# A conformer block, a matrix-memory mixer and a gated recurrence in one kernel: two branches of the mixer in seven-product pairs, its output gates first, some remainders by adding DMAs

## The chip, the cores and the metric

The kernel runs on one core of one Trainium2 chip. The metric is the device time of one execution in microseconds (us), the median of a few runs. TensorE multiplies matrices, VectorE (DVE) and ScalarE (ACT) work element by element, GpSimd (POOL) does a few special steps and issues the adding DMAs, and SyncE (SP) issues most of the other DMAs.

## The reference

512 tokens of width 1024 go through a conformer block (a gated feed-forward layer, a mixer with two kinds of attention, a second feed-forward layer, a norm) and then through two recurrent layers: a matrix-memory mixer (mLSTM, four heads) and a gated linear recurrence. All is float32. The change lies in the matrix memory, of which this is the part that matters (`u` is the normed input):

```python
def mlstm_mixer(u, w_in, conv_w, conv_b, w_q, w_k, w_v, b_i, b_f, norm_w, skip, w_out):
    proj = u @ w_in
    xm, z, o_pre, i_pre, f_pre = jnp.split(proj, [M_INNER, 2 * M_INNER, 3 * M_INNER, 3 * M_INNER + M_HEADS], axis=-1)
    xc = jax.nn.silu(causal_dwconv(xm, conv_w, conv_b))
    # per head of 512 columns: q, k (256 wide) from xc, v (512 wide) from xm
    h_tilde = mlstm_chunkwise(q, k, v, log_i, log_f)
    hh = sigmoid(o_pre) * h_tilde
    hn = layernorm(hh) * norm_w                  # over the 512 columns of a head
    y = (hn + skip * xc) * jax.nn.silu(z)
    return y @ w_out
```

Here `w_in` is 1024 by 6152, so x, z and o take 512 columns each in every one of the four heads.

## The kernel before

Activations lie transposed: a tile holds 128 features by 512 tokens. A float32 product is made of three single-pass ones: each operand is split into a part `hi` that TensorE's fast float32 format holds exactly and a remainder `lo`, and `mm3` (lines 112 to 115) issues hi by hi, hi by lo and lo by hi. A weight is brought by `wload` (lines 93 to 101): SP loads it into `raw` (128 by 1024, four buffers), ScalarE rounds it into `hi` (line 98), VectorE subtracts for `lo` (line 100); `hi` and `lo` have five buffers each. One such load serves 24 matmuls of 512 columns.

The feed-forward layers already use the class `Pair` and `pair_products` (lines 225 to 341). There two groups of 128 output columns are treated as a two-by-two product of blocks and computed with seven block products instead of eight. The inputs' sums come once from `xhalves` and its `step(k)` (lines 266 to 293), which leaves 28 tiles of 128 by 512 to be kept. The weights' sums come for each pair from a DMA that adds (line 214, issued by GpSimd), two VectorE additions (lines 249 and 250) and splits (lines 220, 222, 258, 260). Each of the seven products is 12 matmuls of 256 columns, and VectorE joins them (lines 325 to 337). While one pair is multiplied, the next is loaded and split.

In the matrix memory, `mlstm` (lines 708 to 987), no pairs are used. For each head `z_proj` and `x_proj` run four plain groups each (a group is 24 matmuls of 512 columns), `o_proj` 96 matmuls of 512 columns for the output gate, `v_proj` 48, `qk_proj` 48, `out_proj` 96; `scores` and `numer` are the chunk's attention-like part, `x_conv` the convolution, `y_out` the gating (transposes and elementwise work). The order is written out by hand at lines 960 to 987: head 0 is opened, then each of three passes runs scores, o (or v), numer, z of the next head, y_out, x and v of the next head, x_conv, out_proj (in the third pass o of head 3), q and k; a tail finishes head 3.

A scheduler orders each engine's instructions by this order, by priorities (`tc.high_priority` moves an instruction ahead by so many places) and by when they can run, and gives tiles their buffers. Long-lived tiles come from the pool `ap` (40 buffers), shorter ones from `xp` (18, through `ctile`), and double tiles from `gp` (2, twice as large).

## Time and profile before

| | |
|---|---|
| median of 3 runs | 1811.5 us (1811.38 to 1811.58) |
| the profiled execution's own time | 1811.49 us |
| span of its instructions | 1809.8 us |
| mean granted TensorE clock | 0.998 |

The span runs from the first to the last instruction; 1.7 us of the time lie around it. In the profile an engine's busy time counts the time in which at least one of its instructions runs. TensorE's matmuls overlap, so the distance between two starts tells their pace, and not the duration that is listed for one.

### The profile page before, as it was taken

What the parts mean: (1) busy time and instruction counts of PE and PEld (TensorE: products, weight loads), DVE (VectorE), ACT (ScalarE), POOL (GpSimd) and SP (SyncE); (2) the same over time, 40 slices, a digit from 0 to 9 for tenths busy, and PEclk for the clock granted to TensorE, in tenths of its full rate; (3) what the DMA queues carried; (4) which work ended last, traced back from release to release, by engine and by line L of the source; (5) the groups of instructions that cost most, each with busy time, mean ns of one, the idle gap of its engine ahead of it and who ended that gap; (6) DMA issues with size and microseconds to landing.
All of it is one profiled execution on the core that took longest, in us unless ns stands there. A gap on an engine that the chain in (4) does not pass through costs nothing.

```text
span 1809.8 us, 24643 instructions
## 1 busy us (share of the span) xinstructions
PE 1786.7 (99%) x9640; PEld 1515.3 (84%) x9640; DVE 1244.5 (69%) x1985; ACT 813.6 (45%) x1205; POOL 65.6 (4%) x89
## 2 busy tenths in 40 slices
PE   8999999999999999999999999999999999999998
PEld 6899999887776688799999988888888888888886
DVE  7977777735656465887777766758366566777775
ACT  5443344524345433443444444535334444456662
POOL 1000000000000000010000000000000000000000
PEclk9999999999999999999999999999999999999999
DMA  7466554433322123265556432222222231322312
GB/s 230 116 165 156 149 155 131 139 105 97 102 82 70 47 94 105 69 176 151 153 152 155 118 109 89 71 93 94 77 93 87 70 105 59 102 91 87 99 61 73
DMA packets 74805, 198.10 MB, mean 109 GB/s; under 512 B 8000, under 2 KB 8128, under 8 KB 74688
## 3 DMA queue, kind: packets, MB, share of 16 engines
q1 hardware_dynamic: 63024, 174.35, 30.0%
q0 software_dynamic: 9792, 18.88, 6.5%
q10 hardware_dynamic: 1872, 3.29, 0.6%
q8 instruction: 76, 1.25, 0.3%
q14 instruction: 41, 0.34, 0.1%
HBM read 193.08 MB, written 2.10 MB: 108 GB/s over the span
## 4 chain that ended last, share of the span: by engine, by line
PE 80%; issue 13%; DVE 4%; ACT 1%; DMA 1%; SPq 0%; POOLq 0%; POOL 0%; ACTq 0%; DVEq 0%
PE bank L113 21%; PE bank L114 20%; PE bank L115 20%; PE cbank L113 5%; PE cbank L115 5%; PE cbank L114 5%; PE cbank L635 1%; PE cbank L603 1%; DVE chain L124 1%; PE cbank L909 1%; PE cbank L910 1%; PE cbank L911 1%; DVE act L273 1%; PE cbank L572 0%; PE cbank L942 0%
## 5 line engine op out<-in xcount | busy, mean ns | idle before, releaser
L113 PE MATMUL bank<-act,hi 128*128 128x512 f32 (+1 forms) x1648 | 615.2, 374 | 8.3 <-ACT act L139 7.0
L114 PE MATMUL bank<-act,hi 128*128 128x512 f32 (+1 forms) x1648 | 612.8, 373 | 1.1 <-DVE act L140 1.0
L115 PE MATMUL bank<-act,lo 128*128 128x512 f32 (+1 forms) x1648 | 611.5, 372 | 0.7 <-DVE lo L100 0.7
L98 ACT CAST hi<-raw 128x1024 fp32r<-128x1024 f32 (+2 forms) x210 | 212.3, 1014 | 424.6 <-PE bank L114 193.7
L113 PEld LDWEIGHTS bank<-act,hi 128*128 128x128 f32 x1648 | 310.7, 189 | 67.0 <-ACT act L139 7.0
L114 PEld LDWEIGHTS bank<-act,hi 128*128 128x128 f32 x1648 | 310.9, 189 | 56.4 <-DVE act L140 3.3
L115 PEld LDWEIGHTS bank<-act,lo 128*128 128x128 f32 x1648 | 310.9, 189 | 56.2 <-issue 1.9
L100 DVE TENSOR_TENSOR lo<-raw,hi 128x1024 fp32r<-128x1024 f32 (+2 forms) x210 | 246.6, 1176 | 100.6 <-ACT hi L98 99.7
L220 ACT CAST hi<-raw 128x1024 fp32r<-128x1024 f32 x140 | 146.2, 1050 | 232.0 <-PE cbank L114 107.8
L222 DVE TENSOR_TENSOR lo<-raw,hi 128x1024 fp32r<-128x1024 f32 x140 | 170.8, 1224 | 82.1 <-ACT hi L220 77.7
L113 PE MATMUL cbank<-chain,hi 128*128 128x256 f32 x432 | 122.3, 283 | 1.7 <-ACT hi L220 1.7
L115 PE MATMUL cbank<-chain,lo 128*128 128x256 f32 x432 | 122.3, 283 | 0.9 <-DVE lo L222 0.9
L114 PE MATMUL cbank<-chain,hi 128*128 128x256 f32 x432 | 122.2, 283 | 0.0
L113 PE MATMUL cbank<-act,hi 128*128 128x256 f32 (+1 forms) x264 | 88.2, 334 | 0.0
L114 PE MATMUL cbank<-act,hi 128*128 128x256 f32 (+1 forms) x264 | 87.6, 332 | 0.0
L115 PE MATMUL cbank<-act,lo 128*128 128x256 f32 (+1 forms) x264 | 87.5, 332 | 0.0
L113 PE MATMUL bank<-hi,act 128*128 128x512 f32 x224 | 87.5, 391 | 0.0
L115 PE MATMUL bank<-hi,act 128*128 128x512 f32 x224 | 87.5, 391 | 0.0
L114 PE MATMUL bank<-lo,act 128*128 128x512 f32 x224 | 87.2, 389 | 0.0
L113 PEld LDWEIGHTS cbank<-chain,hi 128*128 128x128 f32 x432 | 82.7, 192 | 3.5 <-ACT hi L220 2.1
L115 PEld LDWEIGHTS cbank<-chain,lo 128*128 128x128 f32 x432 | 82.7, 192 | 1.4 <-DVE lo L222 1.1
L114 PEld LDWEIGHTS cbank<-chain,hi 128*128 128x128 f32 x432 | 82.8, 192 | 1.2
(287 smaller groups left out, 2574.0 us busy)
## 6 DMA issues: line engine op xcount, KB each, us to landing
raw<-in_mh_dram SPq DMA_DIRECT2D x64, 512.0 KB, 3.4
raw<-in_gu_dram SPq DMA_DIRECT2D x52, 512.0 KB, 3.5
raw<-in_gu_dram SPq DMA_DIRECT2D x72, 256.0 KB, 2.9
raw<-in_gu_dram POOLq DMA_DIRECT2D x36, 512.0 KB, 6.0
raw<-in_win_dram SPq DMA_DIRECT2D x34, 512.0 KB, 3.5
raw<-in_dn_dram SPq DMA_DIRECT2D x64, 256.0 KB, 2.9
v<-in_gu_dram SPq DMA_DIRECT2D x36, 256.0 KB, 2.6
raw<-in_mo_dram SPq DMA_DIRECT2D x16, 512.0 KB, 3.4
```

The costliest lines, as they stand in the source:

```text
L98: S.copy(hi[:, :cols], raw[:, :cols])
L100: V.tensor_tensor(lo[:, :cols], raw[:, :cols], f(hi[:, :cols]), op=ALU.subtract)
L113: PE.matmul(ps, st[0], mv[0], start=start, stop=False)
L114: PE.matmul(ps, st[0], mv[1], start=False, stop=False)
L115: PE.matmul(ps, st[1], mv[0], start=False, stop=stop)
L124: V.tensor_tensor(lo, x, f(hi), op=ALU.subtract)
L220: S.copy(hi, raw)
L222: V.tensor_tensor(lo, raw, f(hi), op=ALU.subtract)
L273: V.scalar_tensor_tensor(t, x[i], gain[:, i : i + 1], rb, op0=ALU.mult, op1=ALU.mult)
L603: PE.matmul(ps[:, :n], bq[i][ro, nb * P : nb * P + P], bk[0][ro, b0 * P : b1 * P], start=True, stop=True)
L635: PE.matmul(po[64 * g : 64 * g + 64, :], bv[0][:, kb * P + 64 * g : kb * P + 64 * g + 64], ptc, start=kb == b0, stop=kb == b1 - 1)
L909: PE.matmul(ps[:, :n], wh, vh[:, c0:c1], start=s == 0, stop=False)
```

## The change

Three things are done, all in the matrix memory, and one that touches the pools of the whole kernel.

- z of all four heads (two pairs each) and x of heads 1 to 3 (two pairs each) are computed by `Pair` and `pair_products`, 14 pairs in all, in four runs (`pair_run`): in each pass z, z, then `numer`, then x, x, and after `x_conv` of the third pass z, z of head 3. The inputs' sums are made by `step(k)` after the gates.
- `o_proj` of all four heads runs at the start, one after the other; the gates of heads 1 to 3 are stored to DRAM (`dp`) and loaded again by `o_load` after `scores`.
- The weights of v, q, k and the output product get their remainder in another way (`wload` with `adding`): ScalarE writes minus `hi` into `lo`, and a DMA issued by GpSimd adds the weight from DRAM. They are placed twice as far ahead in priority.
- The pools `ap`, `xp` and `gp` become one pool of 62 tiles; the double tiles become two single ones. `pair_products` now returns its two results, and the feed-forward layers' own part of it moves to `hidden`.

```diff
@@ -46,14 +46,13 @@
 
     cp = ctx.enter_context(tc.tile_pool(name="cp", bufs=1))
     op = ctx.enter_context(tc.tile_pool(name="op", bufs=1))
-    ap = ctx.enter_context(tc.tile_pool(name="ap", bufs=40))
+    ap = ctx.enter_context(tc.tile_pool(name="ap", bufs=62))
     wp = ctx.enter_context(tc.tile_pool(name="wp", bufs=5))
     sp = ctx.enter_context(tc.tile_pool(name="sp", bufs=32))
-    gp = ctx.enter_context(tc.tile_pool(name="gp", bufs=2))
     hp = ctx.enter_context(tc.tile_pool(name="hp", bufs=KD))
     rp = ctx.enter_context(tc.tile_pool(name="rp", bufs=2))
-    xp = ctx.enter_context(tc.tile_pool(name="xp", bufs=18))
     vp = ctx.enter_context(tc.tile_pool(name="vp", bufs=5))
+    dp = ctx.enter_context(tc.tile_pool(name="dp", bufs=12, space=bass.MemoryType.DRAM))
     pp = ctx.enter_context(tc.tile_pool(name="pp", bufs=4, space=PSUM))
     qp = ctx.enter_context(tc.tile_pool(name="qp", bufs=4, space=PSUM))
 
@@ -90,13 +89,17 @@
     mhalf = cp.tile([P, 16], F32, tag="mhalf", name="mhalf")
     G.memset(mhalf, -0.5)
 
-    def wload(src, cols=WU):
-        with tc.high_priority(offset=BOOST):
+    def wload(src, cols=WU, adding=False):
+        with tc.high_priority(offset=BOOST * (2 if adding else 1)):
             raw = wp.tile([P, WU], F32, tag="raw", name="raw", bufs=4)
             nc.sync.dma_start(raw[:, :cols], src)
             hi = wp.tile([P, WU], F32R, tag="hi", name="hi")
             S.copy(hi[:, :cols], raw[:, :cols])
             lo = wp.tile([P, WU], F32R, tag="lo", name="lo")
+            if adding:
+                S.activation(lo[:, :cols], f(hi[:, :cols]), AF.Copy, scale=-1.0)
+                G.dma_start(lo[:, :cols], src, accum_op=ALU.add)
+                return hi, lo
             V.tensor_tensor(lo[:, :cols], raw[:, :cols], f(hi[:, :cols]), op=ALU.subtract)
         return hi, lo
 
@@ -252,11 +255,13 @@
 
         def last(self):
             with tc.high_priority(offset=BOOST):
-                t = vp.tile([P, T + 32], F32, tag="v", name="v")
+                if self.wide:
+                    t = wp.tile([P, WU], F32, tag="raw", name="raw", bufs=4)
+                    hi, lo = (wp.tile([P, WU], F32R, tag=n, name=n) for n in ("hi", "lo"))
+                else:
+                    t, hi, lo = (vp.tile([P, T + 32], dt, tag="v", name="v") for dt in (F32, F32R, F32R))
                 nc.sync.dma_start(t[:, :T], self.low[:, T:])
-                hi = vp.tile([P, T + 32], F32R, tag="v", name="v")
                 S.copy(hi[:, :T], t[:, :T])
-                lo = vp.tile([P, T + 32], F32R, tag="v", name="v")
                 V.tensor_tensor(lo[:, :T], t[:, :T], f(hi[:, :T]), op=ALU.subtract)
             self.w["a22"] = cut((hi, lo), slice(0, T))
 
@@ -319,12 +324,11 @@
         product(c2[:, L], w["s1"], b["t1"])
         product(c2[:, R], w["s3"], b["t3"])
         product(c1[:, R], w["s2"], b["t2"])
-        t = gp.tile([P, 2 * T], F32, tag="four", name="four")
-        v = act_tile()
+        one, two, v = act_tile(), act_tile(), act_tile()
         with tc.high_priority(offset=EVAC):
-            V.tensor_tensor(quarters(t)[:, 0:4:3], quarters(c1), twice(p1[:, L]), op=ALU.add)
-            V.tensor_tensor(quarters(v), quarters(c2), twice(t[:, 3 * HT :]), op=ALU.add)
-            V.scalar_tensor_tensor(t[:, 3 * HT :], c2[:, R], 1.0, v[:, L], op0=ALU.mult, op1=ALU.add)
+            V.tensor_tensor(quarters(one), quarters(c1), twice(p1[:, L]), op=ALU.add)
+            V.tensor_tensor(quarters(v), quarters(c2), twice(one[:, R]), op=ALU.add)
+            V.scalar_tensor_tensor(two[:, R], c2[:, R], 1.0, v[:, L], op0=ALU.mult, op1=ALU.add)
         between(1)
         c3 = bank()
         product(c3[:, L], w["s4"], b["b22"])
@@ -334,8 +338,12 @@
         if nxt:
             nxt.last()
         with tc.high_priority(offset=EVAC):
-            V.tensor_tensor(t[:, HT : 3 * HT], c3, v, op=ALU.add)
-        g, u = t[:, :T], t[:, T:]
+            V.tensor_tensor(one[:, R], c3[:, L], v[:, L], op=ALU.add)
+            V.tensor_tensor(two[:, L], c3[:, R], v[:, R], op=ALU.add)
+        return one, two
+
+    def hidden(pair, b, nxt, between):
+        g, u = pair_products(pair, b, nxt, between)
         S.activation(g, g, AF.Silu)
         V.scalar_tensor_tensor(u, u, -1.0, g, op0=ALU.mult, op1=ALU.mult)
         return split(u)
...
@@ -790,8 +792,42 @@
 
         st = [dict() for _ in range(4)]
 
-        def z_proj(hd):
-            st[hd]["z2"] = [silu2(group(wload(a["mh"][hd][4 + j]), xs), rb) for j in range(4)]
+        b, step = xhalves(x, g0, rb)
+        def pair_of(n, hd, j):
+            m = hd + 1 if n == "x" else hd
+            c = j + (4 if n == "z" else 0)
+            return Pair(a["mh"][m][c], a["mh"][m][c + 1], True)
+
+        def pair_run(jobs):
+
+            cur = pair_of(*jobs[0])
+            cur.load()
+            cur.first()
+            cur.sums()
+            cur.last()
+            for i, (n, hd, j) in enumerate(jobs):
+                if n is None:
+                    hd()
+                    continue
+                more = [q for q in jobs[i + 1 :] if q[0]]
+                nxt = pair_of(*more[0]) if more else None
+                one, two = pair_products(cur, b, nxt, lambda i: None)
+                cur = nxt
+                if n == "z":
+                    S.activation(one, one, AF.Silu)
+                    S.activation(two, two, AF.Silu, scale=-1.0)
+                    st[hd].setdefault("z2", []).extend((one, two))
+                else:
+                    s_ = st[hd + 1]
+                    for t, sign in ((one, 1), (two, -1)):
+                        hi, lo = act_tile(F32R), act_tile(F32R)
+                        S.activation(hi, t, AF.Copy, scale=float(sign))
+                        if sign > 0:
+                            V.tensor_tensor(lo, t, f(hi), op=ALU.subtract)
+                        else:
+                            V.scalar_tensor_tensor(lo, t, -1.0, f(hi), op0=ALU.mult, op1=ALU.subtract)
+                        s_.setdefault("xm", []).append((hi, lo))
+                        s_.setdefault("xr", []).append((t, sign))
 
         def x_proj(hd):
             xm, xr = [], []
...
@@ -817,7 +853,7 @@
             xm = st[hd].pop("xm")
             vps = [bank() for _ in range(4)]
             for kk in range(2):
-                w = wload(a["mh"][hd][14 + kk])
+                w = wload(a["mh"][hd][14 + kk], adding=True)
                 for b in range(4):
                     for j in range(2):
                         k = 2 * kk + j
@@ -838,14 +874,13 @@
             xcs = st[hd].pop("xcs")
             qk = []
             for i in range(2):
-                w = wload(a["mh"][hd][12 + i])
+                w = wload(a["mh"][hd][12 + i], adding=True)
                 w3 = tuple(z.rearrange("p (k m) -> p k m", k=4) for z in w)
-                both = gp.tile([P, 2 * T], F32R, tag="four", name="four")
                 for m in range(2):
                     ps = bank()
                     for k in range(4):
                         mm3(ps, tuple(z[:, k, m * P : (m + 1) * P] for z in w3), xcs[k], k == 0, k == 3)
-                    hi, lo = both[:, m * T : (m + 1) * T], act_tile(F32R)
+                    hi, lo = act_tile(F32R), act_tile(F32R)
                     scale = (1.0 / 16, 1.0)[i]
                     with tc.high_priority(offset=EVAC):
                         S.activation(hi, ps, AF.Copy, scale=scale)
@@ -867,8 +902,18 @@
                 t = ctile()
                 with tc.high_priority(offset=EVAC):
                     S.activation(t, ops[b], AF.Tanh, scale=rsh[:, b : b + 1])
+                if hd:
+                    d = dp.tile([P, T], F32, tag="og", name="og")
+                    nc.sync.dma_start(d, t)
+                    t = d
                 ot.append(t)
             st[hd]["o"] = ot
+
+        def o_load(hd):
+            for b_ in range(4):
+                t = act_tile()
+                nc.sync.dma_start(t, st[hd]["o"][b_])
+                st[hd]["o"][b_] = t
 
         def scores(hd):
             qk = st[hd].pop("qk")
@@ -950,7 +995,7 @@
         def out_proj(hd, o0=0, o1=4):
             ys = st[hd]["y"]
             for o2 in range(o0, o1):
-                w = wload(a["mo"][hd][o2])
+                w = wload(a["mo"][hd][o2], adding=True)
                 for j in range(2):
                     ps = group(w, ys, base=4 * j)
                     o = 2 * o2 + j
@@ -958,27 +1003,32 @@
                         V.tensor_tensor(x[o], ps, x[o], op=ALU.add)
 
         x_proj(0)
-        z_proj(0)
         gate_rows()
         x_conv(0)
-        o_proj(0)
+        for hd in range(4):
+            o_proj(hd)
+        for k in range(4):
+            step(k)
         residual()
+        v_proj(0)
         qk_proj(0)
         for hd in range(3):
+            z = [("z", hd, 0), ("z", hd, 2)]
+            xj = [("x", hd, 0), ("x", hd, 2)]
             scores(hd)
-            (o_proj if hd else v_proj)(hd)
-            numer(hd)
-            z_proj(hd + 1)
+            if hd:
+                o_load(hd)
+            pair_run(z + [(None, lambda: numer(hd), 0)] + xj)
             y_out(hd)
-            x_proj(hd + 1)
             v_proj(hd + 1)
             x_conv(hd + 1)
             if hd < 2:
                 out_proj(hd)
             else:
-                o_proj(3)
+                pair_run([("z", 3, 0), ("z", 3, 2)])
             qk_proj(hd + 1)
         scores(3)
+        o_load(3)
         out_proj(2, 0, 1)
         numer(3)
         out_proj(2, 1, 3)
...
```

## Rows read from the trace of the kernel before

**Rows 1.** The page, parts 1 and 4: busy engines, chain that ended last.

```profile
span 1809.8 us, 24643 instructions
...
PE 1786.7 (99%) x9640; PEld 1515.3 (84%) x9640; DVE 1244.5 (69%) x1985; ACT 813.6 (45%) x1205; POOL 65.6 (4%) x89
...
PE 80%; issue 13%; DVE 4%; ACT 1%; DMA 1%; SPq 0%; POOLq 0%; POOL 0%; ACTq 0%; DVEq 0%
```

**Rows 2.** Timeline of TensorE, a pair, then plain groups: start, duration, what.

```profile
1016.62 0.28 PE L113 MATMUL bank<-act,hi 128*128 128x256 f32 x1
...
1026.68 0.40 PE L113 MATMUL bank<-act,hi 128*128 128x512 f32 x1
...
1291.15 0.39 PE L113 MATMUL bank<-act,hi 128*128 128x512 f32 x1
...
1312.93 1.91 PE L942 MATMUL cbank<-ident,chain 128*128 128x128 f32 x16
1314.59 0.48 PE L113 MATMUL bank<-act,hi 128*128 128x512 f32 x1
```

**Rows 3.** Waits of weight loads, 1125 to 1152 us: total, times, longest.

```profile
PEld bank L113 <- ACT act L122: 0.9, 2, 0.7
...
PEld bank L114 <- DVE act L124: 0.6, 2, 0.4
```

**Rows 4.** Windows: one pass over a head, feed-forward pairs, the step into pairs.

```profile
1258.00:1380.30 122.30, 122.30 (x584) 102.56 (x583) 73.92 (x127) 51.05 (x75) 2.29 (x9) 1.00 0.27 87
85.00:350.00 265.00, 265.00 (x1813) 246.98 (x1813) 203.06 (x259) 112.74 (x145) 16.91 (x14) 1.00 0.57 152
740.00:764.00 24.00, 21.71 (x116) 18.27 (x115) 23.49 (x47) 11.67 (x20) 0.00 (x0) 1.00 0.04 13
```

**Rows 5.** Groups of VectorE by form, the same pass: busy, mean ns, idle before.

```profile
L100 DVE TENSOR_TENSOR lo<-raw,hi 128x1024 fp32r<-128x1024 f32 x20 | 24.4, 1222 | 16.8 <-ACT hi L98 16.7
...
L1009 DVE SCALAR_TENSOR_TENSOR act<-act,vec 128x510 f32<-128x510 f32 x4 | 3.0, 750 | 0.1
...
L945 DVE SCALAR_TENSOR_TENSOR act<-cbank,nwh,act 128x512 f32<-128x512 f32 x4 | 2.9, 744 | 0.0
...
L202 DVE TENSOR_TENSOR act<-bank,rb 128x512 f32<-128x512 f32 x4 | 2.8, 690 | 8.0 <-PE bank L115 8.0
...
L1006 DVE TENSOR_SCALAR act<-act,vec 128x512 f32<-128x512 f32 x4 | 2.2, 539 | 0.0
```

**Rows 6.** Groups of VectorE by form, feed-forward pairs (85 to 350 us).

```profile
L222 DVE TENSOR_TENSOR lo<-raw,hi 128x1024 fp32r<-128x1024 f32 x60 | 73.4, 1225 | 38.2 <-ACT hi L220 36.1 <-DMA v<-in_gu_dram 2.1
...
L326 DVE TENSOR_TENSOR act<-cbank,four 128x512 f32<-128x512 f32 x17 | 11.7, 691 | 0.6
...
L249 DVE TENSOR_TENSOR raw<-raw 128x512 f32<-128x512 f32 x15 | 10.4, 692 | 0.5
...
L327 DVE SCALAR_TENSOR_TENSOR four<-cbank,act 128x256 f32<-128x256 f32 x17 | 7.2, 424 | 0.5
```

**Rows 7.** Waits of weight loads at the step into pairs (745 to 770 us).

```profile
PEld cbank L113 <- ACT hi L220: 1.1, 1, 1.1
PEld cbank L115 <- DVE lo L222: 1.1, 1, 1.1
PEld bank L113 <- ACT hi L220: 0.6, 1, 0.6
```

**Rows 8.** The weights' casts on ScalarE, whole program, by form.

```profile
L98 ACT CAST hi<-raw 128x1024 fp32r<-128x1024 f32 x170 | 178.5, 1051 | 379.0 <-PE bank L114 166.1 <-issue 129.6 <-PE bank L115 45.1
```

**Rows 9.** The page, part 3: DMA queue, packets, MB, share of 16 engines.

```profile
q1 hardware_dynamic: 63024, 174.35, 30.0%
q0 software_dynamic: 9792, 18.88, 6.5%
```

**Rows 10.** Line 214, the adding DMA: duration ns min/median/max; time to landing.

```profile
L214 POOL DMA_DIRECT2D raw<-in_gu_dram x36: 1203/1203/1378, 27.5 to 990.6; - x36
...
DMA to landing us min/median/max: 5.6/6.0/8.3
```

More of the change, by code (lines that the diff above doesn't have):

```diff
@@ L38 @@
 NVEC = _n
-PAD = 478
+PAD = 414
 @with_exitstack
@@ L66, in ctile @@
     def ctile(dt=F32):
-        return xp.tile([P, T], dt, tag="chain", name="chain")
+        return ap.tile([P, T], dt, tag="act", name="chain")
     def cbank():
@@ L225, with __init__ @@
     class Pair:
-        def __init__(self, top, low):
-            self.top, self.low, self.w = top, low, {}
+        def __init__(self, top, low, wide=False):
+            self.top, self.low, self.w, self.wide = top, low, {}, wide
         def load(self):
@@ L397, in ffn @@
             job(-1)
-            new.append(pair_products(cur, b, nxt, job))
+            new.append(hidden(cur, b, nxt, job))
             cur = nxt
@@ L444, in rope_tables @@
         def rope_tables():
-            both = gp.tile([P, 2 * T], F32, tag="four", name="four")
             for i in range(2):
-                t = both[:, i * T : (i + 1) * T]
+                t = act_tile()
                 S.dma_start(t, a["rope"][i])
@@ L481, in vb_group @@
             bv.append(vb)
-        room = []
         def gate(i):
             ps = group(wload(win[i]), xs)
-            if i < 20:
-                if not room:
-                    room.append(gp.tile([P, 2 * T], F32, tag="four", name="four"))
-                g = room[0][:, (i - 18) * T : (i - 17) * T]
-            else:
-                g = act_tile()
+            g = act_tile()
             with tc.high_priority(offset=EVAC):
@@ L735, in mlstm @@
         rb = rows(rs)
+        neg = cp.tile([P, 64], F32, tag="neg", name="neg")
+        V.tensor_scalar(neg, vc("mcw", 0, 64), -1.0, None, op0=ALU.mult)
         nwh = cp.tile([P, 16], F32, tag="nwh", name="nwh")
@@ L808, in x_conv @@
             xc2, xcs = [], []
-            for j, t in enumerate(st[hd].pop("xr")):
-                c = conv(t, "mcw", 16, "mcb", 4 * hd + j)
+            for j, (t, sign) in enumerate(st[hd].pop("xr")):
+                c = conv(t, "mcw", 16, "mcb", 4 * hd + j, neg if sign < 0 else None)
                 S.activation(c, c, AF.Silu)
```

12 lines of the change are left out of this document (8 added, 4 removed).

## The prediction

> **What bounds the kernel now.** I read the page first: TensorE is busy 99% of the span, VectorE 69%, ScalarE 45%, and the chain of waits is TensorE for 80% and issue for 13%, which is mostly the same matmuls between their records [rows 1]. So the time is the number of matmuls times their pace, plus the few places where TensorE waits. Then the timeline gives the pace. The two halves of a feed-forward pair have no other work between them: 84 matmuls of 256 columns from 1016.62 to 1026.68 us, so 10.06 us a pair, or 0.120 us each. The four z groups of a later head are 96 matmuls of 512 columns from 1291.15 to 1312.93, so 21.78 us, or 0.227 us each [rows 2]. A matmul of half the columns costs 53% of the time, not 50%. Then the waits: inside the matrix memory the weight loads waited almost only around 1125 to 1152 us, where head 0's q and k follow close on its convolution [rows 3]. In one pass over a head (122.3 us) TensorE has no gap, its granted clock is 1.00 (the upper of its two levels), VectorE is busy 73.9 us and ScalarE 51.1 [rows 4]. What the change does to TensorE is therefore a matter of count and pace; what it does to VectorE decides whether the pace is kept.
>
> **TensorE.** Two output groups cost 48 matmuls of 512 columns, 48 x 0.2269 = 10.89 us; a pair costs 10.06 us. That is 0.83 us a pair, and 14 x 0.83 = **-11.6 us**. The matmuls of the gates are only moved. The Trainium skill (TensorE: Matmul & The Clock Gate, Back-to-back issue gap) gives a stream N / 2.4 + 2.5 ns for N columns; by it two groups would cost 48 x 215.8 ns, a pair 84 x 109.2 ns, and the 14 pairs would gain 16.6 us, an estimate. The trace shows 226.9 and 119.8 ns, so about 11 ns more for every matmul, and the scheme that has more matmuls pays that more often; I keep -11.6.
>
> **Head 0's opening.** The waits there are 0.9 us for ScalarE's splits of the convolved input and 0.6 us for VectorE's [rows 3]. After the change four `o_proj` (4 x 96 x 0.2269 = 87 us) and `v_proj` stand between `x_conv` and `qk_proj`: **-1.5 us**. In the same 87 us VectorE has the 16 remainders of the gates' weights (16 x 1.222 = 20 us), the convolution and the four `step(k)`; in the feed-forward layer the steps kept VectorE busy for most of 24 us [rows 4]. With the convolution (13.9, below) that is under 60 of 87 us, so the steps are covered; without that cover they would cost up to their 24 us. The last steps may have to wait for tiles that the gates' input gives back only during the last `o_proj`; behind that come `v_proj`, `qk_proj` and `scores`, over 25 us of TensorE, before a pair needs them. Hence nothing.
>
> **VectorE in a pass.** All 20 remainders of a pass go (8 of z and x, 8 to the adding DMAs, 4 with the gates): 20 x 1.222 = 24.4 us. So do 8 scalings out of PSUM, 8 x 0.690 = 5.5 [rows 5]. Each pair brings three wide remainders (3 x 1.225), one narrow one and two sums (3 x 0.69), two joins of 512 columns (2 x 0.69) and three of 256 (3 x 0.424): 8.4 us, four pairs 33.6 us [rows 6]. So 73.9 - 30 + 33.6 = 77.5 us, in a pass that shrinks from 122.3 by the gate (96 x 0.2269 = 21.8) and four pairs (3.3) to 97.2 us: 80% instead of 60%. In the feed-forward pairs VectorE is busy 203.06 of 265 us, 77%, and TensorE keeps 100% there [rows 4]. So I cost the steady state at nothing; the cover is 19.7 us of VectorE's idle time in a pass, and beyond it each us is a us of the kernel.
>
> **The starts of the four runs.** The first pair of a run has no pair before it under which it is split. In the feed-forward layer that first step cost 1.1 + 1.1 + 0.6 = 2.8 us [rows 7], with VectorE busy 23.49 of 24 us ahead of it [rows 4]. The bounds are 0 and 2.8 us for each of four. Ahead of these starts VectorE is at about 80%, nearer to the 77% that cost nothing than to 98%; I take a third, 0.9 us: **+3.6 us**.
>
> **The tight place.** In the third pass z of head 3 stands where `o_proj` was. Between the x pairs and `qk_proj(3)` TensorE has 16 transposes (1314.59 - 1312.93 = 1.7 us [rows 2]), `v_proj` (48 x 0.2269 = 10.9) and two pairs (20.1): 32.7 us. VectorE has `y_out`, 4 x (0.744 + 2 x 0.69) = 8.5; v's remainders, 2.8; the convolution with its splits, 4 x (0.539 + 3 x 0.75 + 0.69) = 13.9; and two pairs, 16.8 [rows 5, 6]: 42.0 us. That is 9.3 us too much, of which the first pair's splits and sums (5.7) can be done before: 3.6 us. If the scheduler puts part of `out_proj(2)` forward, nothing is lost. Bounds 0 and 9.3, likely part 0 to 3.6; the half, **+1.8 us**.
>
> **The adding DMAs.** The 32 weights cost VectorE nothing now; ScalarE makes two passes instead of one. The cast of this shape is 1.05 us [rows 8]; the pass with a factor isn't in the trace, and I take the same. ScalarE in a pass: 51.1 less 12 casts of z, x and o (12.6), plus 4 x 3.5 casts for the pairs (14.7), four small copies and 8 extra passes (8.4), about 63 of 97 us; hidden. A weight is then ready 1.05 + 1.05 + 6.0 = 8.1 us after its buffer is free (landing 5.6 to 8.3) [rows 10]. With five buffers a weight of `out_proj` has some four groups of 5.4 us to do it. The shortest lead is `v_proj`'s first weight, whose buffer the pair before last gives back: one pair and the transposes, 10.06 + 1.7 = 11.7 us. So it fits, by 3.6 us at the median and 1.3 at the longest landing. The queues: the plain one moved 174.35 MB in 30.0% of the span (321 GB/s while busy), the adding one 18.88 MB in 6.5% (160 GB/s) [rows 9], so one add of 0.524 MB takes 3.3 us of all engines. A pass has 12 adds (39 us) and 10.5 MB of plain loads (8 weights of 0.524, four pairs of 1.31, the gate's 1.05: 33 us): 74% of 97 us, where the pass before shows 27% and the feed-forward pairs 57% [rows 4]. Costed at nothing, with less room than elsewhere.
>
> **DRAM and pools.** The gates' 12 stores and 12 loads of 256 KB lie far from their use: z pairs of 20 us follow each load. SP waits for the tanh before a store, and weights queue behind it; about three loads are ahead by priority (75 places, some 29 instructions a load), so some 14 us of matmuls. One shared pool can shorten or lengthen the feed-forward starts (2.8 us each in the worst): 0, bounds -4 and +4.
>
> **Sum.** -11.6 - 1.5 + 3.6 + 1.8 = -7.7 us. The profiled execution took 1811.49 us (span 1809.8), the median is 1811.5, so the difference carries over: **1803.8 us**. With starts and the tight place free it is 1798.4; with both dear (11.2 and 3.6) 1813.2.
>
> **Rivals.**
> - *VectorE becomes the bound of the three passes (slower).* Price: a pass takes 77.5 us divided by the share that VectorE reaches. The 13.1 us gained are 4.4 a pass, so it turns slower once the share stays under 77.5 / 101.6 = 76%. At 74% a pass takes 104.7 us, 22.5 in all, and the time is about 1821. For it: its queue is in order and idles 8 to 17 us a pass behind ScalarE and TensorE now [rows 5], and 23.49 of 24 us busy did cost TensorE 2.3 us [rows 4]. Against it: 77% with TensorE full.
> - *The adds come late (no change).* If each `v_proj` waits for one more add in front of it (3.3 us), and the first of `out_proj` likewise behind a GpSimd queue that runs in order, three passes cost 10 us: 1814. For it: 74% of DMA time and a lead of 11.7 us. GpSimd's queue also holds the masks of `scores` (line 891) and the power of `numer` (line 931), which wait for ScalarE and VectorE, and an add placed behind one of them waits too. Against: leads of 20 us elsewhere.
> - *GpSimd is held up while it writes the adds' descriptors.* The lead of `v_proj` allows a landing of 11.7 - 2.1 = 9.6 us. The landings spread over 2.7 us (5.6 to 8.3); if VectorE's load adds that spread once more to the longest, 11.0 us, each of three passes waits 1.4 us: +4.2, 1808. Against it: 36 issues at 1203 to 1378 ns and landings at 5.6 to 8.3 us [rows 10], while VectorE was 77% busy. [...]
> - *Everything hides and the larger pool also removes the feed-forward starts' waits:* 1798.4 less up to 4, about 1796.
>
> **Chances.** The forecast 0.60, VectorE as bound 0.16, late adds 0.13, GpSimd held 0.03, everything hidden 0.08. About 0.2% (3.6 us) is what a measurement can tell from no change, so faster is under 1807.9 and slower over 1815.1. Of the forecast's 0.60 some 0.54 lies under 1807.9; with 0.08 and 0.01 that is 0.63 faster. The rest of the forecast, most late adds and the held GpSimd make 0.20 the same; VectorE and the late adds' tail 0.17 slower. The range leaves out VectorE's case and the best of the hidden one: 1797.5 to 1814. The forecast's own range is 1798.4 to 1813.2.
>
> **What would show it.** Right: the page counts 504 more matmuls (10144), 14 pairs in the matrix memory at 10.06 us from first to last start, a pass of about 98 us with VectorE at 76 to 80%, no waits at `qk_proj(0)`, waits of about 1 us at a run's start. Wrong: weight loads that wait on `lo` for the add in `v_proj` or `out_proj`; on VectorE's remainders (line 222's) in the middle of a run; on the convolution before `qk_proj(3)`; a pass over 101.6 us; or a changed feed-forward layer.

## The result, and the profile after

The changed kernel takes 1892.8 us (1891.5 to 1895.2), 1.045 times the kernel before (95% interval 1.043 to 1.047): 81.3 us slower, where 7.7 us faster was forecast. The profiled execution took 1892.95 us. The page of the changed kernel, parts 1, 4 and 3, answers to [rows 1, 9]:

```profile
span 1891.1 us, 26248 instructions
...
PE 1803.1 (95%) x10144; PEld 1549.5 (82%) x10144; DVE 1289.8 (68%) x2128; ACT 879.6 (47%) x1295; POOL 112.9 (6%) x135
...
q1 hardware_dynamic: 70512, 184.32, 30.9%
q0 software_dynamic: 18208, 43.00, 13.3%
...
PE 71%; issue 14%; DVE 7%; DMA 4%; ACT 3%; POOL 0%; SPq 0%; POOLq 0%; ACTq 0%; DVEq 0%
```

The count of matmuls is the predicted 10144. TensorE's share fell from 99 to 95%. In the chain that ended last the shares of VectorE, DMA and ScalarE rose from 4, 1 and 1% to 7, 4 and 3%. The steady state is what was predicted; first the two x pairs of the first pass (timeline of TensorE), then the passes from one head's scores to the next (windows: length, busy time and count of TensorE, weight loads, VectorE, ScalarE and GpSimd, granted clock, DMA share, GB/s):

```profile
1281.63 0.28 PE L116 MATMUL bank<-act,hi 128*128 128x256 f32 x1
...
1301.79 0.82 PE L987 MATMUL cbank<-ident,chain 128*128 128x128 f32 x6
```

```profile
1252.50:1351.70 99.20, 97.99 (x630) 88.50 (x630) 75.43 (x143) 60.16 (x88) 15.00 (x21) 1.00 0.64 158
1351.70:1453.60 101.90, 99.71 (x635) 90.32 (x634) 75.92 (x143) 59.31 (x87) 14.93 (x21) 0.98 0.67 167
```

Two pairs took 20.16 us, 10.08 each, as in [rows 2]; a pass took 99.2 and 101.9 us instead of 122.3 [rows 4]. The time was lost elsewhere. I added up over all matmuls by how much each starts later than the pace of the one before it allows (0.227 us for 512 columns, 0.120 for 256; only lags over 0.06 us), and call these the lags. Some 45 us of that sum, most of it in the attention between 400 and 650 us, is in every kernel and only a misfit of this simple pace. The columns are stretches of the span in us; "rest" is the time from the first matmul to the last less the lags:

| kernel | 0–1050 us | opening 1050–1260 | to 1440 | to 1650 | recurrence | sum | rest |
|---|---|---|---|---|---|---|---|
| before | 45.0 | 3.2 | 0.7 | 0.9 | 1.2 | 51.0 | 1743.7 |
| changed | 51.0 | 45.9 | 6.0 | 20.1 | 22.4 | 145.4 | 1732.5 |
| e1_pools | 50.8 | 24.9 | 0.9 | 6.2 | 21.3 | 104.0 | 1743.7 |
| e12_scal | 44.9 | 47.2 | 5.7 | 22.6 | 1.2 | 121.6 | 1733.4 |
| e13_best2 | 45.5 | 8.5 | 2.9 | 15.5 | 1.2 | 73.5 | 1733.0 |
| e10_shift | 43.5 | 2.6 | 0.7 | 0.7 | 0.7 | 48.2 | 1769.6 |

The rest fell by 11.2 us: the pairs earn what they should. The lags rose by 94.4 us. (The two make 83.2 us; the other 2 us of the difference lie before the first matmul and after the last.) Of the 94.4 us 42.7 lie in the opening of the matrix memory, nearly all of it two waits and the lower clock behind them (waits of weight loads, 1100 to 1260 us: total, times, longest), where [rows 3] had 1.5 us:

```profile
PEld bank L116 <- DVE act L868: 19.5, 1, 19.5
PEld bank L116 <- ACT chain L904: 16.8, 1, 16.8
```

The first, on ScalarE's timeline (start, duration, what; the idle time before it in brackets). Line 847 is the Silu of head 0's convolution, line 904 the tanh that empties the four PSUM banks of the first `o_proj`:

```profile
1116.78 0.63 ACT L847 ACTIVATE act<-act 128x512 f32<-128x512 f32 x1
...
1124.74 0.63 ACT L847 ACTIVATE act<-act 128x512 f32<-128x512 f32 x1 [2.09 <-DVE act L1064]
...
1129.59 0.63 ACT L847 ACTIVATE act<-act 128x512 f32<-128x512 f32 x1 [2.09 <-DVE act L1064]
...
1134.44 0.63 ACT L847 ACTIVATE act<-act 128x512 f32<-128x512 f32 x1 [2.09 <-DVE act L1064]
...
1135.63 2.41 ACT L904 ACTIVATE chain<-bank,small 128x512 f32<-128x512 f32 x4
```

The banks are full at 1119.5. But the tanh stands behind four Silus, each of which waits for VectorE's convolution, and the second `o_proj` needs the same four banks. The second wait, on VectorE's timeline (line 283 belongs to the steps, line 868 is v's remainders):

```profile
1206.19 0.43 DVE L283 TENSOR_TENSOR act<-act 128x256 fp32r<-128x256 f32 x1 [24.86 <-ACT act L282]
...
1233.45 2.48 DVE L868 TENSOR_TENSOR act<-bank,v 128x512 fp32r<-128x512 f32 x4
```

VectorE idles 24.9 us on the first step, then does all four steps and the residual for 27 us, and only then v's remainders, while the four banks of `v_proj` stay taken from 1214.7 on. The first step waited for its cast on ScalarE (line 282), which runs behind the tanh of the fourth gate:

```profile
1204.23 0.69 ACT L904 ACTIVATE chain<-bank,small 128x512 f32<-128x512 f32 x1 [0.67 <-PE bank L118]
...
1205.75 0.41 ACT L282 CAST act<-act 128x256 fp32r<-128x256 f32 x1
```

So none of the steps' casts ran under the four gate products that were to cover them.

Each long wait costs some more at its end, as the windows of the two waits and of the 10 us after each show:

```profile
1119.50:1136.50 17.00, 0.42 (x4) 0.18 (x2) 12.59 (x18) 7.74 (x13) 0.00 (x0) 0.64 0.15 56
1136.50:1146.50 10.00, 10.00 (x35) 8.02 (x36) 1.02 (x1) 3.21 (x5) 0.00 (x0) 0.77 0.01 2
...
1214.70:1234.00 19.30, 0.37 (x2) 0.00 (x0) 19.29 (x37) 7.54 (x13) 0.00 (x0) 0.63 0.10 28
1234.00:1244.00 10.00, 9.81 (x31) 7.89 (x32) 3.42 (x7) 1.71 (x3) 0.00 (x0) 0.69 0.08 26
```

The granted clock is 0.77 and 0.69 there; the first matmuls start every 0.427 us (the lower of the two levels) instead of 0.227, and 35 and 31 starts in 10 us instead of 44 cost about 2 and 3 us.

The other waits: the end of the third pass (1500 to 1600 us; line 318 is the copy of a pair's first product), the recurrence (1660 to 1885), and the step into pairs (745 to 770), which answers to [rows 7]:

```profile
PEld bank L116 <- ACT chain L318: 5.2, 1, 5.2
PEld bank L116 <- DVE act L868: 4.4, 1, 4.4
PEld cbank L987 <- DVE act L979: 1.5, 1, 1.5
...
PEld bank L116 <- ACT act L125: 8.5, 4, 3.2
PEld cbank L174 <- DVE chain L169: 4.2, 1, 4.2
PEld bank L117 <- DVE act L127: 1.9, 2, 1.2
...
PEld cbank L116 <- ACT act L125: 2.3, 1, 2.3
PEld cbank L116 <- ACT chain L125: 1.1, 1, 1.1
PEld cbank L117 <- DVE chain L127: 0.5, 1, 0.5
```

The two longest of the third pass have queues behind them too. Ahead of the first, ScalarE stood idle 7.9 us on a cast (line 223) for the fourth run's first pair, whose add landed after 11.7 us, with the splits of x for `v_proj` (line 824) behind it. VectorE, which waited 5.9 us for those splits, then did the gating of `y_out` before v's remainders (line 868), and the fourth run waited 4.4 us for v's bank. The second, 5.2 us, is the copy of line 318, which stood behind the whole convolution (line 847), as the tanh does in the opening:

```profile
1508.75 1.05 ACT L223 CAST hi<-raw 128x1024 fp32r<-128x1024 f32 x1 [7.88 <-DMA raw<-in_mh_dram]
1509.70 1.14 ACT L824 ACTIVATE act<-act 128x512 fp32r<-128x512 f32 x2
...
1546.87 0.62 ACT L847 ACTIVATE act<-act 128x512 f32<-128x512 f32 x1
...
1548.51 0.37 ACT L318 COPY chain<-bank 128x256 f32<-128x256 f32 x1
```

Nothing of the recurrence's code was changed. What changed for it is the pool of its tiles.

### The profile page after: what moved, and what is told of

It is laid out like the page before. It is cut to its first block, busy times and chain, and to the rows that moved or that the text cites. A ratio compares the mean times of both kernels' runs of the same rounds, so it can differ in the third digit from the quotient of the medians.

```text
span 1891.1 us, 26248 instructions
## 1 busy us (share of the span) xinstructions
PE 1803.1 (95%) x10144; PEld 1549.5 (82%) x10144; DVE 1289.8 (68%) x2128; ACT 879.6 (47%) x1295; POOL 112.9 (6%) x135
## 4 chain that ended last, share of the span: by engine, by line
PE 71%; issue 14%; DVE 7%; DMA 4%; ACT 3%; POOL 0%; SPq 0%; POOLq 0%; ACTq 0%; DVEq 0%
PE bank L116 17%; PE bank L117 17%; PE bank L118 17%; PE cbank L116 5%; PE cbank L117 5%; PE cbank L118 5%; DMA raw<-in_mh_dram 2%; DVE lo L225 1%; PE cbank L635 1%; DVE chain L127 1%; DVE act L278 1%; DMA lo<-in_mo_dram 1%; DVE act L127 1%; PE cbank L603 1%; DMA lo<-in_mh_dram 1%
## 5 line engine op out<-in xcount | busy, mean ns | idle before, releaser
L116 PE MATMUL bank<-act,hi 128*128 128x512 f32 (+1 forms) x1536 | 564.2, 368 | 41.5 <-DVE act L868 23.1
L117 PE MATMUL bank<-act,hi 128*128 128x512 f32 (+1 forms) x1536 | 562.7, 367 | 1.4 <-DVE act L127 0.9
L118 PE MATMUL bank<-act,lo 128*128 128x512 f32 (+1 forms) x1536 | 560.6, 365 | 0.0
L223 ACT CAST hi<-raw 128x1024 fp32r<-128x1024 f32 x182 | 190.7, 1049 | 282.6 <-PE bank L117 121.6
L225 DVE TENSOR_TENSOR lo<-raw,hi 128x1024 fp32r<-128x1024 f32 x182 | 222.1, 1224 | 105.5 <-ACT hi L223 101.3
L103 DVE TENSOR_TENSOR lo<-raw,hi 128x1024 fp32r<-128x1024 f32 (+2 forms) x150 | 173.4, 1158 | 68.0 <-ACT hi L97 66.8
L116 PE MATMUL cbank<-chain,hi 128*128 128x256 f32 x600 | 171.3, 286 | 2.3 <-ACT chain L125 1.8
L117 PE MATMUL cbank<-chain,hi 128*128 128x256 f32 x600 | 171.2, 285 | 0.7 <-DVE chain L127 0.7
L118 PE MATMUL cbank<-chain,lo 128*128 128x256 f32 x600 | 171.0, 285 | 0.0
L116 PEld LDWEIGHTS cbank<-chain,hi 128*128 128x128 f32 x600 | 116.7, 195 | 4.5 <-ACT chain L125 2.2
L117 PEld LDWEIGHTS cbank<-chain,hi 128*128 128x128 f32 x600 | 116.5, 194 | 2.4 <-DVE chain L127 1.1
L116 PE MATMUL bank<-hi,act 128*128 128x512 f32 x224 | 89.3, 398 | 17.1 <-ACT chain L904 16.6
L127 DVE TENSOR_TENSOR act<-act 128x512 fp32r<-128x512 f32 x96 | 66.2, 689 | 40.3 <-ACT act L125 40.1
L125 ACT CAST act<-act 128x512 fp32r<-128x512 f32 x96 | 59.5, 620 | 69.7 <-DVE act L348 34.2
```

The costliest lines, as they stand in the source:

```text
L103: V.tensor_tensor(lo[:, :cols], raw[:, :cols], f(hi[:, :cols]), op=ALU.subtract)
L116: PE.matmul(ps, st[0], mv[0], start=start, stop=False)
L117: PE.matmul(ps, st[0], mv[1], start=False, stop=False)
L118: PE.matmul(ps, st[1], mv[0], start=False, stop=stop)
L125: S.copy(hi, x)
L127: V.tensor_tensor(lo, x, f(hi), op=ALU.subtract)
```

## The experiments

**One part alone: the shared pool.** The kernel before with one pool of 62 tiles, the double tiles cut in two and the joins of the feed-forward pairs with them (the pools alone are shown):

```diff
-    ap = ctx.enter_context(tc.tile_pool(name="ap", bufs=40))
-    gp = ctx.enter_context(tc.tile_pool(name="gp", bufs=2))
-    xp = ctx.enter_context(tc.tile_pool(name="xp", bufs=18))
+    ap = ctx.enter_context(tc.tile_pool(name="ap", bufs=62))
```

> The kernel before with only the pools changed: one pool of 62 tiles for all, double tiles as two single ones, and the joins of the pair as in the changed kernel. Theory (the shared pool costs about a third of the loss, through the order of work in the feed-forward starts and in the recurrence behind the matrix memory): slower than before by 20 to 32 us, about 1837 us, with the added waits at 50 to 65, 755 to 770 and after 1690 us of the span. Rival (the loss lies in the matrix memory alone, the waits elsewhere follow from its lateness): 1811 us, within 3 us of before.

1864.0 us, +52.3 (ratio 1.0286, 1.027 to 1.030). The part that I had costed at nothing is the largest (the parts overlap, so they do not add up to 81.3). Beside the recurrence (+20.1) and the starts, it shows the wait of the changed kernel's opening in a kernel that has neither pairs nor moved gates (weight loads, 1100 to 1170 us; line 861 is the tanh):

```profile
PEld bank L111 <- ACT chain L861: 16.5, 1, 16.5
```

In its ScalarE queue the tanh stands behind all four Silus; in the kernel before it stands behind two. ScalarE's timeline, first of the kernel before (line 811 the Silu, line 869 the tanh), then of e1 (lines 804 and 861):

```profile
1125.79 0.63 ACT L811 ACTIVATE act<-act 128x512 f32<-128x512 f32 x1
...
1129.43 0.69 ACT L869 ACTIVATE chain<-bank,small 128x512 f32<-128x512 f32 x1
...
1133.98 0.62 ACT L811 ACTIVATE act<-act 128x512 f32<-128x512 f32 x1
```
```profile
1157.39 0.63 ACT L804 ACTIVATE act<-act 128x512 f32<-128x512 f32 x1 [2.09 <-DVE act L1001]
...
1158.57 2.41 ACT L861 ACTIVATE chain<-bank,small 128x512 f32<-128x512 f32 x4
```

So the one shared pool, with its cut tiles, changes the order in which the instructions are laid into the queues. The number of bytes is the same (40 + 18 + 2 double ones); what is new is that all tiles share one pool.

**Two places in the order.** The changed kernel with the convolution behind the second `o_proj` (e2), and with v, q and k ahead of the steps (e3):

```diff
+        for hd in range(2):
+            o_proj(hd)
         x_conv(0)
-        for hd in range(4):
+        for hd in range(2, 4):
             o_proj(hd)
```
```diff
+        v_proj(0)
+        qk_proj(0)
         for k in range(4):
             step(k)
         residual()
-        v_proj(0)
-        qk_proj(0)
```

> The changed kernel with the convolution of head 0 issued after the second of the four gate products instead of ahead of the first. Theory (the gate's tanh stood behind the convolution's Silu in ScalarE's queue, and the second gate product waits for the four banks that the tanh empties): the wait of 16.7 us at 1119 us goes, and the time falls by 14 to 17 us, to about 1877 us. Rival (VectorE is simply late there, so the wait moves to the later gate products or to q and k): falls by less than 5 us.

> The changed kernel with the four steps of the inputs' sums and the residual issued after v and q, k of head 0 instead of ahead of them. Theory (v's remainders stood behind some 27 us of steps and residual in VectorE's queue, and q and k wait for the banks): the wait of 19.3 us at 1215 us goes, a wait of 3 to 10 us comes at the first pair, and the time falls by 9 to 16 us, to about 1880 us. Rival (the steps are late by what VectorE lacks, so the whole wait moves to the first pair): within 4 us of the changed kernel.

e2: 1878.4, 14.4 us less than the changed kernel; the wait at the tanh shrank from 16.8 to 3.1. e3: 1896.4, 3.6 us more. The wait at v went, and came back where the pairs need the steps (weight loads, 1200 to 1270 us):

```profile
PEld bank L116 <- ACT act L282: 13.1, 4, 4.3
PEld cbank L116 <- DVE chain L938: 3.7, 1, 3.7
```

So in the changed kernel the first wait is a place in a queue. The second is also work without cover: in this order the steps come too late for the pairs.

**No adding DMAs** (`adding=True` taken out everywhere):

> The changed kernel with no adding DMAs for v, q, k and the output weights: VectorE makes their remainders as before. Theory (the adds cost 2 to 5 us by late landings and by ScalarE's second pass, and VectorE has room for 32 remainders of 1.2 us): faster than the changed kernel by 0 to 8 us, about 1889 us. Rival (VectorE is the bound of the passes, and the adds relieve it): slower by 10 us or more, over 1903 us.

1892.0, 0.9 less, with overlapping ranges: this run's four times spread over 9.4 us, so a few us either way can't be seen. The adds are not free where they are late. In the changed kernel four weight loads wait 4.2 us for one; the longest, at the second pass's `v_proj` (1260 to 1500 us), has eight matmuls at the lower clock behind it and so costs about 4 us. Without the adds these waits go (some 3 us of lags from 1260 to 1440 us instead of 6.0), but the wait at the copy of line 318 in the third pass grows from 5.2 to 10.2 us. The adds of line 101 also landed later than the 5.6 to 8.3 us of [rows 10]. First that longest wait, then the time to landing (line 101):

```profile
PEld bank L117 <- DMA lo<-in_mh_dram: 2.4, 1, 2.4
...
DMA to landing us min/median/max: 5.5/10.7/14.5
```

**Pools per block** (44 and 18 tiles for the conformer block and the recurrence, 62 for the matrix memory):

```diff
+    open_pools(62)
     mlstm(h)
+    open_pools(44, 18)
     rglru(h)
```

> The changed kernel with its tiles opened per block: 44 + 18 in two pools for the conformer block and for the recurrence, one pool of 62 for the matrix memory alone. Theory (the shared pool lets the instruction order of the other blocks slip): the start of the two feed-forward layers falls from 6.6 and 7.5 us of TensorE's waits to about 2 and 3.5, the recurrence from 22.4 to 1 to 3, so 26 to 30 us less than the changed kernel, 1863 to 1867; the matrix memory keeps its waits of 16.7 and 19.3 us. Rival (those waits come from the joins in two halves and the double tiles split in two, which stay): no change, 1888 to 1895.

1890.5: the rival's band, and yet the sum of the lags fell by 29.8 us, as the theory said. The rest had grown by 22.5 us: every stream of matmuls of 512 columns ran at 0.233 us instead of 0.227. The new pools began 640 bytes past a multiple of 2048 (by the pools' sizes; the traces hold no addresses). Four runs tested that: e12 is e5 with the pools on a multiple again, e10 is the kernel before with its pool of activations 640 bytes off and nothing else, e15 and e16 the same with 128 and 1024 bytes (and v's tiles moved with them).

```diff
-    ap = ctx.enter_context(tc.tile_pool(name="ap", bufs=40))
...
     vp = ctx.enter_context(tc.tile_pool(name="vp", bufs=5))
+    ap = ctx.enter_context(tc.tile_pool(name="ap", bufs=40))
```

> e5_scoped (the changed kernel with pools per block and nothing else) with the activation tiles on a multiple of 2048 bytes. Theory of e5_scoped with the pace put right: 1863 to 1868. Rival (the pools were not the cause of the starts' and the recurrence's waits, or the pace stays): 1885 to 1893.

> The kernel before, with one line moved: the pool of its activation tiles is opened after that of v, so that these tiles begin 640 bytes past a multiple of 2048 and the others stay on multiples. Nothing else differs. Theory (place of the moving operand): the matmuls of 512 columns take 0.233 us, some 4,400 x 6 ns, 1832 to 1842. Rival (the place doesn't matter): 1810 to 1814.

> e10_shift with 128 bytes in place of 640 past a multiple of 2048 for the activation tiles (v's tiles move by 128 too). If any place off a multiple of 2048 bytes costs 6.3 ns a matmul of 512 columns: 1834 to 1838. If only places off a coarser or another grid count (640 = 512 + 128, 128 alone does not): 1810 to 1814.

> e10_shift with 1024 bytes in place of 640 past a multiple of 2048. If what counts is a multiple of 1024 or less: 1810 to 1814. If it is 2048: 1834 to 1838.

e10: 1835.9 (+24.4), e15: 1835.1 (+23.6), e16: 1811.6 (0.0; ratio 0.999 to 1.001). Two matmuls of e10, 23 starts apart:

```profile
1639.75 0.40 PE L114 MATMUL bank<-act,hi 128*128 128x512 f32 x1
...
1645.12 0.39 PE L113 MATMUL bank<-act,hi 128*128 128x512 f32 x1
```

5.37 / 23 = 0.2335 us. e12: 1871.4, 21.5 us less than the changed kernel, 3 us above what was expected and far from the rival. The joins in two halves and the cut tiles stayed in e5 and e12, so for the blocks outside the matrix memory it is the sharing of one pool that cost (by both kinds of tiles and by all blocks; e12 undoes the two at once). The waits of the recurrence and the step into pairs are those of the kernel before again (745 to 770, then 1660 to 1885 us):

```profile
PEld cbank L131 <- ACT hi L238: 1.1, 1, 1.1
PEld cbank L133 <- DVE lo L240: 1.1, 1, 1.1
PEld bank L131 <- ACT hi L238: 0.6, 1, 0.6
...
PEld bank L133 <- DVE lo L118: 0.8, 1, 0.8
PEld bank L132 <- DVE act L142: 0.6, 2, 0.4
PEld bank L131 <- ACT act L140: 0.4, 1, 0.4
```

**The third pass and the opening.** e6 orders the opening anew, e7 moves z of head 3 between scores(3) and numer(3), e8 has both and the pools per block, e9 is e8 on a multiple of 2048. The order of e6, and the place in e7:

```diff
         gate_rows()
+        o_proj(0)
         x_conv(0)
-        for hd in range(4):
-            o_proj(hd)
+        v_proj(0)
+        qk_proj(0)
+        scores(0)
+        o_proj(1)
+        numer(0)
         for k in range(4):
             step(k)
+        o_proj(2)
+        o_proj(3)
         residual()
-        v_proj(0)
-        qk_proj(0)
```
```diff
-                pair_run([("z", 3, 0), ("z", 3, 2)])
+                out_proj(2, 0, 2)
             qk_proj(hd + 1)
         scores(3)
         o_load(3)
-        out_proj(2, 0, 1)
+        pair_run([("z", 3, 0), ("z", 3, 2)])
         numer(3)
-        out_proj(2, 1, 3)
+        out_proj(2, 2, 4)
         y_out(3)
-        out_proj(2, 3, 4)
```

> The changed kernel with another opening of the matrix memory: o_proj(0) ahead of the convolution of head 0, then v_proj, qk_proj, scores, o_proj(1), numer, the steps, o_proj(2), o_proj(3) and the residual; the first pass then has its four pairs without a pause. Theory (both waits of the opening are places in in-order queues: ScalarE's tanh behind the convolution's Silu, VectorE's remainders of v behind the steps): both waits go, 16.7 + 19.3 us less and up to 5 us of new small waits, 1857 to 1864. Rival (VectorE has too much to do in the opening, so that wherever the steps stand something waits for them): the wait of 19 us comes back as several, 1872 to 1880.

> The changed kernel with the two z pairs of head 3 moved out of the third pass, to between scores(3) and numer(3); half of out_proj(2) takes their place ahead of qk_proj(3), the other half stands after numer(3). Theory (the third pass is dear since VectorE has the convolution, v's remainders and two pairs in 33 us of TensorE): of the 14 to 15 us of waits from 1503 to 1592 some 9 to 13 go, 1880 to 1884. Rival (the start of the run is what costs, wherever it stands): 1889 to 1894.

> The changed kernel with the three edits before at once (pools per block, the other opening, z of head 3 late). Theory (the places are independent of each other, and the seven-product pairs gain their 0.83 us each): the waits fall to near those of the kernel before, 1804 to 1816. Rival (something common to them, the DMA or VectorE's load, sets the passes): over 1825.

> The kernel of all three edits (e8_all), with the pools placed so that the activation tiles begin at a multiple of 2048 bytes again, as in the kernels before and after; in e5_scoped and e8_all they began 640 bytes past one. In both of those the matmuls of 512 columns started every 0.233 us, not 0.227, everywhere in the program, and the waits of TensorE are 30 and 40 us shorter than in the changed kernel while the time fell by only 2.4 and 17. Theory (the place of the moving operand sets this pace): some 3,700 matmuls x 6.3 ns less, 1850 to 1855. Rival (the pace has another cause in the kernels with pools per block): 1872 to 1878.

e6: 1877.6 (-15.3), the rival's band: the convolution lost its cover, and `qk_proj` waited 13.7 us. The profile names no releaser for it; the wait ended at 1145.3 us, when VectorE, done with the convolution, came to v's remainders (line 868, from 1144.5) and emptied the first bank. e7: 1888.5 (-4.3), between the two. e8: 1875.8, and 40 us less of lags than the changed kernel. e9: 1852.8, 23.0 us under e8, as the place of the tiles would have it. On e9 builds e11: v ahead of the gates, the convolution under `o_proj(1)`, two steps on either side of numer, the residual in the first pass, v's weights without adds, the z pairs of head 3 on both sides of numer(3).

> The three edits, aligned, with the opening ordered anew (v_proj(0), o_proj(0), convolution, o_proj(1), qk_proj, scores, two steps, o_proj(2), numer, two steps, o_proj(3), residual after the first z pairs), v's weights split by VectorE and not by adding DMAs, and the two z pairs of head 3 on both sides of numer(3). Theory (what is left of the waits are places in the in-order queues of the opening, 14 + 8 us, and adds that come 2.5 us late three times): 30 us under e9_aligned, 1812 to 1828. Rival (each cure moves the wait elsewhere, as e3_steps did): 1840 to 1855.

1832.1, between the two. Its largest wait (4.4 us) was for the transposes of `gate_rows`, which had `v_proj` alone as cover; e13 moves them:

```diff
         x_proj(0)
-        gate_rows()
         v_proj(0)
+        gate_rows()
         o_proj(0)
         x_conv(0)
         o_proj(1)
         qk_proj(0)
         scores(0)
```

> e11_best with gate_rows behind v_proj(0), so that its transposes fall among the matmuls of o_proj(0). Theory (the 7.9 us of waits at 1101 to 1110 us were those transposes, waiting for VectorE's small operations with v_proj alone as cover): 6 to 8 us less, 1824 to 1827. Rival (the convolution then ends later and qk_proj waits instead): 1830 to 1836.

1823.2 us (ratio 1.0064, 1.005 to 1.008), 69.6 less than the changed kernel and the best with pairs. The opening's lags are down to 8.5 us. Most of what is left lies in the third pass (weight loads, 1440 to 1570 us):

```profile
PEld bank L131 <- ACT act L140: 5.7, 3, 2.4
PEld bank L131 <- ACT chain L333: 2.6, 1, 2.6
PEld bank L131 <- ACT act L157: 2.0, 1, 2.0
```

**Two misses.** e14 is e1 with the convolution behind `o_proj(0)`; e17 is e13 with the z pairs of head 3 at the end of the third run, behind y_out(2) and the convolution of head 3.

> The kernel before with the shared pool alone (e1_pools), and the convolution of head 0 issued behind o_proj(0). Theory (the 16.4 us wait of e1_pools is the order on ScalarE: the tanh behind the four Silus of the convolution): 14 to 17 us less than its 1864.0, 1847 to 1850. Rival (tiles of the shared pool come free late, wherever the convolution stands): 1860 to 1866.

> e13_best2 with the z pairs of head 3 at the end of the third pass's run of pairs (behind y_out(2) and the convolution of head 3), so that there are three runs of pairs and not four; out_proj(2) is spread as before. Theory (the extra start and the small covers of the tail cost 10 of the 15 us): 1811 to 1817. Rival (VectorE's work between the x pairs and qk_proj(3) costs it, as the prediction's tight place had it): 1820 to 1828.

e14: 1864.0, no change, and so the rival's band. The wait at the tanh went from the opening, but `o_proj(0)` had been the cover of the convolution: `qk_proj` now waited 10.6 us in four pieces for its splits (8.9 for ScalarE's, 1.7 for VectorE's) and `numer` 3.3, and the opening's lags stayed at 24.4 us (24.9 in e1). This shows that the place of the tanh made that wait, not that the order is all: tiles that come free late, which was the rival, were not tested by themselves. e17: 1840.6, 17.4 us slower than e13, above both expectations. ScalarE's copy of the first product (line 333) and VectorE's joins stood behind the whole convolution (1475 to 1496 us), so that `v_proj` found no free bank:

```profile
PEld bank L131 <- ACT chain L333: 15.2, 1, 15.2
```

It is the same mechanism as at the start, made by hand: taking an extra start away is worth little if a 20 us chain goes in front of the pairs' own small operations.

## Why the prediction was wrong, step by step

- *TensorE, -11.6:* right. 10.08 us a pair, and the rest fell by 11.2 us. The 16.6 us estimated from the Trainium skill's page (TensorE: Matmul & The Clock Gate, Back-to-back issue gap) are not borne out. That section also gives 131 ns for a matmul of 512 columns in a stream with weight loads; the 227 ns of this trace differ from that figure still more.
- *Head 0's opening, -1.5:* the named waits, for the splits of the convolved input, went. But the step counted TensorE time as cover and didn't look at what shares an in-order queue with what. Each gate product needs its banks emptied by the tanh: 16.8 us behind the Silus, and about 2 more of lower clock. e2 shows that the place of the convolution makes this wait (-14.4). But e1 has it too (16.5 us), with one gate product at its old place; so it is as much the fault of the pool step below. Four gate products in a row with the old pools were not run.
- *The steps, "Hence nothing":* the largest single wait, 19.5 us plus some 3 of clock. The text held the steps covered by the 87 us of gate products, expected at most the last of them to wait for tiles of the gates' input, and took the 25 us of TensorE behind them as cover. In the run already the first step's cast came after the last gate's tanh (1205.75 us), so nothing of the steps but the first scaling was covered. Whether a tile or a place in ScalarE's queue held that cast is not shown. Nor did the text see that v's remainders stand behind the steps on VectorE. That is the question "what is queued behind the waiting instruction", unasked at this place. Exchanging the two (e3) only moves the wait; e13, which gives the steps two gate products as cover, has 8.5 us of lags in the whole opening.
- *DRAM and pools, "0, bounds -4 and +4":* failed, +52.3 alone (e1). This is the largest error of the prediction. Pools were weighed as room, and only at the feed-forward starts. Their sharing also changes the order in the queues, in every part of the kernel: in the changed kernel +21.2 us in the recurrence and +6.0 before the matrix memory, in e1 also +21.7 in the opening and +5.3 from 1440 to 1650 us. e12 takes the two outer ones back, and so shows them; inside the matrix memory no run divided the pool again. In the recurrence too ScalarE and VectorE work in another order than before, but that this order, and not tiles that come free late, makes the waits there is not shown. The range of the forecast held nothing of these bounds.
- *VectorE in a pass, nothing:* right. 75.4 us busy of 99.2, 76% (77.5 and 80% forecast). The second pass took 101.9 us, over the 101.6 that the prediction named as a sign of being wrong, but not by VectorE (75.9 us busy): 4 us of it are the late add.
- *The starts, +3.6:* right for the first three runs, whose starts have 0.3 to 0.9 us of lags each (0.9 forecast); the fourth start is in the next point.
- *The tight place, +1.8, bounds 0 and 9.3:* the place was right, the size was not. The third pass and its end have 19.2 us more of lags. In the trace some 14 of them are the two waits shown above, 4.4 and 5.2 us, with the lower clock behind each. The step compared sums of VectorE's and TensorE's work; but ScalarE's queue stands behind both waits, and VectorE itself idled for splits of ScalarE in that stretch (5.9 us before line 826, 5.3 before line 127). Taking z of head 3 away brought 4.3 (e7), as other waits came; in e13, without that place, 15.5 are left, which lie at the convolution's splits ahead of `qk_proj(3)` and at the start of the run. Of its bound of 9.3 us the step took only 3.6 into the range.
- *The adding DMAs, nothing:* right in the sum (e4, -0.9, within its spread), in part by luck. The landing time was wrong: 10.7 us at the median and up to 14.5, where 5.6 to 8.3 were taken and 9.6 was the room at `v_proj`. The prediction's sign of late adds came: four weight loads waited 4.2 us in all for an add in `v_proj` and `out_proj`, and one late add of a pair (11.7 us) stood ahead of the wait at the fourth run's start; how much of that wait it made is not shown. GpSimd's issue did not grow longer: the 82 adds were issued in 954 to 1213 ns on average (lines 101 and 217). What made the landings longer is not shown.

The rivals had the sign of VectorE's case and not its cause: VectorE kept its pace; it and ScalarE did things in the wrong order. What stays open: no version with pairs beat the kernel before. e13's rest is 10.7 us under it and its lags 22.5 us over it, and no run took those last waits away.

## What to carry to other kernels

Cost a moved or merged piece by its place in each in-order queue: for every PSUM bank that is to be emptied, ask which slow chain stands in front of the instruction that empties it. How the tiles are divided into pools is part of the schedule wherever they are used, so run the pool change by itself first, and look at the parts that the diff does not touch. When a run contradicts its own waits, compare the plain pace of the matmuls before doubting the theory.

## What the runs showed of the hardware

- The place of a tile in SBUF sets TensorE's pace. With activation tiles 640 or 128 bytes past a multiple of 2048, matmuls of 512 columns that read them as either operand start every 0.233 us and not 0.227, +24 us in all (e10, e15); at 1024 bytes nothing changes (e16). Those of 256 columns, and those of 512 in e10 whose operands both lay on multiples, keep their 0.119 to 0.120 and 0.227 us. Of the places in between only 640 was tried.
- The long waits of TensorE cost more than their length. In the 10 us after the waits of 16.8 and 19.5 us the granted clock was 0.77 and 0.69, with matmuls of 512 columns first every 0.427 us (the lower level, 1.2 GHz): 2 and 3 us on top. After the 2.4 us wait of the second pass eight matmuls ran at that pace too, 1.6 us more.
- The landing of an adding DMA is no constant: 5.6 to 8.3 us in the kernel before, 5.5 to 14.5 for the adds of v, q, k and the output weights here.
